# Second layer of a two-layer mixer on one core: both halves of a split operand as one moving operand of 512 columns, and the bank evacuated by a ScalarE copy

## The chip, the cores and the metric

The kernel runs on one core of a Trainium2 chip. The metric is the time of one execution in microseconds on the device; the kernel before has a median of 1196.91 us over three runs (1196.71 to 1197.09). Beside these runs one execution was profiled, and every row below is from that execution. Its granted TensorE clock is 1.0 in every slice, the 2.4 GHz level.

## The reference

Two layers of a diffusion backbone run over 256 latent and 256 context tokens of width 2048. In each layer the modulated RMS norm of the tokens goes through one input projection, whose columns are split among two branches and their gates; the gated branches are joined and go through one output projection. Only the latent stream leaves, so the context stream of the second layer is used for keys and values alone. Cut to what matters here, for the latent tokens of one layer:

```
h = rms_norm(x) * (1 + scale) + shift
u, v, za, q, k, vv, zb = split(h @ w_in)
a = gelu(u) * (w_sgu @ rms_norm(gelu(v)) + b_sgu) * silu(za)      # position mixing in chunks of 128
b = softmax(rope(norm(q)) @ rope(norm(k)).T / sqrt(128)) @ vv * silu(zb)   # 8 query heads, 2 key heads
x = x + gate * (concat(a, b) @ w_out)
```

## The kernel before

All large products are float32 products made of float32r passes: each operand is split into `hi` (its value rounded to float32r) and `lo` (what remains), and a product is three passes, hi by hi, hi by lo and lo by hi, that add up in one PSUM bank (`three`, lines 339 to 341).

A *job* is 512 output columns of a projection. Its weights come in 8 pieces of 256 rows by DMA; ScalarE makes a piece's `hi` (L202), VectorE its `lo` (L205), three pieces ahead of their use. In a job of kind "tok" tokens are the output's partitions; in a job of kind "feat", feature-major, 128 features are the partitions, the weights are the stationary operand and the tokens the moving one. The second layer's last part works on the 256 latent tokens alone, so its "feat" jobs move 256 columns per pass. There are ten such jobs: six of the input projection, with which the gates are made (U0, U1 with gelu, ZA0, ZA1, ZB0, ZB1 with silu, in the order U0, ZA0, U1, ZA1, ZB0, ZB1, other jobs between), and four of the output projection. In each, every piece gives four feature blocks (fb 0 to 3) of two contraction steps. The moving operand is the modulated input `h1` in the gate jobs and the gated product `mx` in the output jobs.

The four feature blocks of a job have one PSUM bank each, from a pool of four, so that the next job's block takes the bank of the same number when that has been read. When a gate job's block is complete, `gate_evac` has ScalarE read the bank with the activation (L637) into a tile `act`, and a tick later VectorE multiplies the branch's buffer by it (L642). When an output job's block is complete, VectorE adds it, times the gate, to the residual `x1` from the bank (L975), and a tick later the result leaves by DMA.

Side work runs between the units of the jobs: `tick()` is called after two feature blocks (or one tile of tokens) and moves each task one step on; `later(k, f)` puts f's instructions k + 1 ticks further on. The tasks are the attention of the second layer, the modulation vectors on VectorE (L284), and the position mixing. Attention turns the queries (`qT`, split at L475 and L476), makes scores `s` (TensorE), their negative maximum `nmx` (VectorE, L534), the exponentials `p` (ScalarE, L537, with the sum `sm`), scales p by the reciprocal of the sum (ScalarE, L630), turns it (`tp`, TensorE L544), splits it into `pt` (L475, L476), and multiplies it with the values (`o`, TensorE).

The order of instructions on each engine is that in which this program writes them, and every engine works through its own in order. Tiles of [128, 512] that live shortly (`act`, the split queries qT, p, squares, modulated rows) are taken in turn from one pool, tag "t2", of five buffers: a tile that takes a buffer waits until all readers of its previous tile are done.

Of the kernel before, what the change touches and what calls it, by code (L numbers as in the profile page):

```python
# [63 lines left out]
def mixer_kernel(ctx: ExitStack, tc: tile.TileContext, a, out):  # L64
    """Tokens are ordered latent (tiles 0, 1), context (tiles 2, 3).

    Every large product runs as three float32r passes over exact splits of both
    operands: v = hi + lo with hi = float32r(v), and a*b = hi*hi + hi*lo + lo*hi.
    """
# [67 lines left out]
    # the conditioning vectors behind their SiLU, in rows: (quarter, stream, element)  # L137
# [23 lines left out]
    def consts_task(l, L):  # L161
        """What the mixer needs beside the modulation: norm weights, and those of queries and keys with the rotation."""
# [34 lines left out]
    def split_piece(rs, at_once, mem=None):  # L197
        """float32r parts of two contraction blocks; the second part follows a tick later unless at once."""
        n = rs.shape[1]
        hi = hlp.tile([P, 2, 512], F32R, tag="hi", name=nm("hi"))[:, :n] if mem is None else mem[:, 0]  # L200
        lo = hlp.tile([P, 2, 512], F32R, tag="lo", name=nm("lo"))[:, :n] if mem is None else mem[:, 1]
        S.copy(hi, rs)  # L202

        def rest():
            V.tensor_tensor(out=lo, in0=rs, in1=hi.bitcast(F32), op=ALU.subtract)  # L205
        if at_once:
            rest()
        else:
            later(0, rest)
        return hi, lo  # L210

    class ModItems:
        """Shift and scale of n blocks of features from block kt0, for both streams, on the tensor engine: four
        steps over the contraction, then a finish."""
# [41 lines left out]
    def mod_task(row0, ng, ns, pace, finish):  # L256
        """ng groups of 256 columns of the modulation product on the vector engine, columns on the partitions.
        finish gets the sums [P, 2 * ng, ns] of the first ns streams."""
# [42 lines left out]
    def mod_rest():  # L301
        """The gates of the first layer, then the second layer's modulation."""
        yield from mod_task(0, 8, 2, MOD_PACE[0], mod_gate(L0, 2))
        yield from mod_task(D, 16, 2, MOD_PACE[1], lambda tot: mod_ab(L1, tot[:, :KT], tot[:, KT:], 0, KT))
        yield from mod_task(3 * D, 8, 1, MOD_PACE[2], mod_gate(L1, 1))

# [1 line left out]
    # A task is a generator; it yields how many units of the main stream pass before it goes on.  # L308
# [5 lines left out]
    def later(k, f):  # L314
        """Emit f's instructions k + 1 ticks from now."""
        def once():
            f()
            return
            yield
        spawn(once(), k)  # L320
# [21 lines left out]

    class Job:
        """512 output columns: units of main-stream work for each piece of two contraction blocks."""

        def __init__(self, W, col0, kind, n, operand, evac, order=(0, 1, 2, 3), pre=None, post=None, heavy=False):
            self.W, self.col0, self.kind, self.n = W, col0, kind, n
            self.operand, self.evac, self.order = operand, evac, order
            self.pre, self.post, self.heavy = pre, post, heavy
            self.ps = {}  # L350

        def units(self, i, pc):
# [13 lines left out]
            for fb in range(4):  # L366
                if first:
                    self.ps[fb] = accp.tile([P, 512], F32, tag="acc", name=nm("acc"))
                ps = self.ps[fb][:, :self.n]
                fs = slice(fb * P, (fb + 1) * P)  # L370
                for k in range(2):
                    three(ps, (pc[0][:, k, fs], pc[1][:, k, fs]), self.operand(kt0 + k),
                          first and k == 0, last and k == 1)
# [9 lines left out]
    class Stream:  # L383
        """The pieces of a list of jobs in order, loaded and split ahead of their use."""
# [50 lines left out]
    def head_norm(q, n, kind):  # L435
        """q [P, n, 128] in place: divide by the root mean square of each head."""
# [41 lines left out]
    def attention_task(L, kv, qa, units, done):  # L478
        """kv [P, 4, 512]: k heads in columns 0..255, v heads in 256..511. qa[hf] [P, nt, 4, 128]: queries in,
        transposed attention output in the same place."""  # L480
# [152 lines left out]
    def gate_evac(func, buf, ntok, mix=None):  # L633
        """buf [P, nt, 4, 128] *= func(product), block fb of 128 features; split if that was the last factor."""
        def f(fb, ps):
            t_ = t2([P, 512], "act")[:, :ntok]
            S.activation(t_, ps, func)  # L637
            b = buf[:, :, fb, :]


# [4 lines left out]
            later(0, mul)  # L645
        return f

    def to_mix(buf, mix, fb):
        """Split block fb of a finished [P, nt, 4, 128] buffer into float32r parts [P, 4, tokens]."""
# [6 lines left out]
    def sgu_v(L, buf, hf, nt):  # L656
        """buf [P, nt, 4, 128] gets the position-mixed value path, transposed."""
# [57 lines left out]
    def modulate(L, kt, stream, xs, rb, hi, lo):  # L715
        """hi + lo = xs * rb * A + B for one block of 128 features; returns what makes lo."""
# [7 lines left out]
    # column starts of the combined projection  # L724
    U0, VS0, ZA0, Q0, KV0, ZB0 = 0, 1024, 2048, 3072, 4096, 4608

    # ================= layer 0 =================
# [5 lines left out]
    def mod_load():  # L733
        """Loads modulation weights ahead, into at most MOD_AHEAD buffers."""
# [22 lines left out]
    def stats(s, g):  # L757
        """Mean squares of a stream's tokens; the tensor engine adds up over the features on the partitions."""
# [51 lines left out]
    def rows_h(gi):  # L810
        """Space for the modulated rows of a group, and the steps that make them."""
# [33 lines left out]
    def first_group():  # L845
        """The latent tokens' products run while the other stream arrives."""
# [114 lines left out]
    # the residual stream is read again for the output projection  # L961
# [42 lines left out]
    # layer 1 jobs  # L1004
# [4 lines left out]
    def rhs1(kt):  # L1009
        return h1[0][kt // 8][:, kt % 8, :], h1[0][2 + kt // 8][:, kt % 8, :]  # L1010

    def lhs1(kt, tt):
        hh = h1[tt // NLAT]
        ts = slice((tt % NLAT) * P, (tt % NLAT + 1) * P)
        return hh[kt // 8][:, kt % 8, ts], hh[2 + kt // 8][:, kt % 8, ts]
# [29 lines left out]
    def gate_job1(col0, func, buf, g=None):  # L1045
        def ev(fb, ps):
            assert ("sgu", 1, col0 // 512 % 2) in emitted or col0 >= ZB0
            if g is not None and fb == 0:
                assert g < 2 or g - 2 in done1
                t_ = big([P, 2, 4, SEQ], F32R, s="mx")  # L1050
                MX[g] = (t_[:, 0], t_[:, 1])
# [3 lines left out]
    def mix1(kt):  # L1055
        return MX[kt // 4][0][:, kt % 4, :], MX[kt // 4][1][:, kt % 4, :]

    def out_job1(cn):
        def ev(fb, ps):
            kt = 4 * cn + fb  # L1060
            xs = resid(L1, kt, 0, ps)
            later(0, lambda: nc.sync.dma_start(out=out[kt * P:(kt + 1) * P, :], in_=xs))
        return Job(a["w_out"][1], 512 * cn, "feat", SEQ, mix1, ev)
# [19 lines left out]
    # last columns of layer 0: the latent tokens end first, so that their next layer can begin  # L1083
# [18 lines left out]
    def next_task(s):  # L1102
        """The next layer's input of one stream, from the new residual stream."""
# [19 lines left out]
        for kt in range(KT):  # L1123
            if kt % 8 == 0:
                hs[kt // 8] = big([P, 8, SEQ], F32R, s="h1")
                hs[2 + kt // 8] = big([P, 8, SEQ], F32R, s="h1")
            assert ("mod", D) in emitted
            nxt = modulate(L1, kt, s, x1[s][kt // 8][:, kt % 8, :], rb, hs[kt // 8][:, kt % 8, :],
                           hs[2 + kt // 8][:, kt % 8, :])
# [37 lines left out]
    # ================= layer 1 =================  # L1167
# [6 lines left out]
def _layout(inputs):  # L1174
# [22 lines left out]
    # constants of the shapes alone  # L1197
# [33 lines left out]
```

## Time and profile before

| what | value |
|---|---|
| median of three runs | 1196.91 us |
| profiled execution, own time | about 1196.9 us: span and 2.3 us around it |
| span of the profile | 1194.6 us |
| TensorE busy | 1169.5 us, 98% of the span, 6656 matmuls and turns |
| VectorE busy | 908.9 us, 76% |
| ScalarE busy | 521.5 us, 44% |
| GpSimd busy | 47.0 us, 4% |

The span is the time from the first to the last instruction in the profile. Busy time of an engine says how much of the span its instructions cover; on TensorE consecutive matmuls overlap, so the distance of two starts, not one matmul's duration, is what a matmul costs in a stream. The second layer's "feat" jobs end at about 930 (U0), 961 (ZA0) and 1023 us (U1) while attention runs beside them, and follow each other without it from about 1045 us to the end.

### The profile page before, as it was taken

To read this page: it belongs to the slowest core of one execution; us is meant where nothing else is said; L and a number is where in the kernel's file an instruction comes from. 1 tells how busy PE (TensorE), PEld (TensorE's weight loads), DVE (VectorE), ACT (ScalarE), POOL (GpSimd) and SP (SyncE) were. 2 spreads that over 40 slices of the span, in tenths; PEclk is the share of its full clock that TensorE was granted. 3 is DMA by queue.
4 is the path that set the end of the run, shared out by engine and by line. 5 is a ranking of instruction groups with operands and counts; after the bars stand their busy time and mean duration, and the time that the engine had idled before them with its cause. 6 is when DMAs were issued, how large, how long until landed. Compare 5 with 4: busy or idle time off the path is not lost.

```text
span 1194.6 us, 18034 instructions
## 1 busy us (share of the span) xinstructions
PE 1169.5 (98%) x6656; PEld 991.5 (83%) x6656; DVE 908.9 (76%) x1930; ACT 521.5 (44%) x992; POOL 47.0 (4%) x48
## 2 busy tenths in 40 slices
PE   4999999999999999999999999999999999999998
PEld 2566667888888888888888888987888989999998
DVE  5767769878887777989988998778558687767544
ACT  4422225565555432242332232146366777645332
POOL 1000001011000000010100000000011000000000
PEclk9999999999999999999999999999999999999999
DMA  9986772446354657677786666646456666677752
GB/s 334 345 291 246 264 290 99 145 130 191 117 159 141 178 179 224 192 232 219 253 299 215 215 203 195 229 118 220 139 161 200 216 195 220 207 258 252 236 190 89
DMA packets 132184, 247.52 MB, mean 207 GB/s; under 512 B 8912, under 2 KB 19696, under 8 KB 132096
## 3 DMA queue, kind: packets, MB, share of 16 engines
q1 hardware_dynamic: 130880, 242.08, 62.3%
q0 software_dynamic: 1216, 4.29, 1.0%
q8 instruction: 52, 0.85, 0.3%
q14 instruction: 36, 0.29, 0.1%
HBM read 244.23 MB, written 2.11 MB: 206 GB/s over the span
## 4 chain that ended last, share of the span: by engine, by line
PE 89%; DVE 4%; ACT 3%; issue 1%; SPq 1%; POOL 1%; DMA 1%; POOLq 0%; ACTq 0%; DVEq 0%
PE acc L339 27%; PE acc L341 26%; PE acc L340 26%; PE mod L234 2%; PE tp L544 1%; DVE lo L205 1%; PE sg L686 1%; PE s L341 1%; ACT hi L202 1%; PE o L340 1%; PE o L341 1%; PE o L339 1%; POOL rs L429 1%; PE s L340 1%; PE s L339 1%
## 5 line engine op out<-in xcount | busy, mean ns | idle before, releaser
L202 ACT CAST hi<-raw 128x1024 fp32r<-128x1024 f32 (+1 forms) x242 | 250.7, 1036 | 395.6 <-PE acc L340 283.2
L205 DVE TENSOR_TENSOR lo<-raw,hi 128x1024 fp32r<-128x1024 f32 (+1 forms) x242 | 292.2, 1208 | 126.8 <-ACT hi L202 126.5
L284 DVE SCALAR_TENSOR_TENSOR junk<-raw,scb 128x512 f32<-128x512 f32 x448 | 308.1, 688 | 14.5 <-DMA raw<-in_w_modt 5.5
L339 PE MATMUL acc<-hh,hi 128*128 128x512 f32 x384 | 152.6, 397 | 0.0
L341 PE MATMUL acc<-hh,lo 128*128 128x512 f32 x384 | 149.8, 390 | 0.0
L340 PE MATMUL acc<-hl,hi 128*128 128x512 f32 x384 | 149.8, 390 | 0.0
L339 PE MATMUL acc<-hi,hh 128*128 128x512 f32 x320 | 131.0, 409 | 3.1 <-ACT hh L720 3.1
L341 PE MATMUL acc<-hi,hl 128*128 128x512 f32 x320 | 125.6, 393 | 0.0
L340 PE MATMUL acc<-lo,hh 128*128 128x512 f32 x320 | 125.3, 392 | 0.0
L339 PE MATMUL acc<-h,hi 128*128 128x256 f32 x384 | 110.3, 287 | 1.0 <-ACT s L660 1.0
L341 PE MATMUL acc<-h,lo 128*128 128x256 f32 x384 | 108.6, 283 | 0.0
L340 PE MATMUL acc<-h,hi 128*128 128x256 f32 x384 | 108.5, 283 | 0.0
L339 PE MATMUL acc<-mh,hi 128*128 128x512 f32 (+1 forms) x304 | 106.5, 350 | 0.0
L341 PE MATMUL acc<-mh,lo 128*128 128x512 f32 (+1 forms) x304 | 106.4, 350 | 0.0
L340 PE MATMUL acc<-ml,hi 128*128 128x512 f32 (+1 forms) x304 | 106.4, 350 | 0.0
L339 PEld LDWEIGHTS acc<-hi,hh 128*128 128x128 f32 x320 | 60.5, 189 | 38.8 <-issue 14.7
L341 PEld LDWEIGHTS acc<-hh,lo 128*128 128x128 f32 x384 | 72.1, 188 | 15.4
L340 PEld LDWEIGHTS acc<-hl,hi 128*128 128x128 f32 x384 | 72.3, 188 | 13.5
L339 PEld LDWEIGHTS acc<-hh,hi 128*128 128x128 f32 x384 | 72.2, 188 | 13.5
L429 POOL TENSOR_TENSOR rs<-rs,nhalf 128x4 f32<-128x4 f32 (+1 forms) x36 | 40.9, 1137 | 892.7 <-DVE rs L428 892.7
L340 PE MATMUL acc<-lo,h 128*128 128x512 f32 x192 | 75.3, 392 | 0.7 <-DVE lo L205 0.3
L339 PE MATMUL acc<-hi,h 128*128 128x512 f32 x192 | 75.7, 394 | 0.0
(163 smaller groups left out, 2166.6 us busy)
## 6 DMA issues: line engine op xcount, KB each, us to landing
raw<-in_w_in SPq DMA_DIRECT2D x173, 512.0 KB, 4.4
raw<-in_w_modt SPq DMA_DIRECT2D x128, 512.0 KB, 4.7
raw<-in_w_out SPq DMA_DIRECT2D x64, 512.0 KB, 5.0
raw<-in_w_mod SPq DMA_DIRECT2D x58, 512.0 KB, 6.2
scb<-crow SPq DMA_DIRECT2D x12, 512.0 KB, 6.0
xT<-in_xT SPq DMA_DIRECT2D x8, 512.0 KB, 7.8
x<-in_xT POOLq DMA_DIRECT2D x4, 1024.0 KB, 11.0
mod<-in_w_mod SPq DMA_DIRECT2D x6, 512.0 KB, 7.7
```

What stands on the lines that cost most here:

```text
L202: S.copy(hi, rs)
L205: V.tensor_tensor(out=lo, in0=rs, in1=hi.bitcast(F32), op=ALU.subtract)
L234: T.matmul(self.ps[32 * j:32 * j + 32, :wd], sc[:, 4 * g + j, :], self.raw[g][j], start=(g == 0), stop=(g == 3))
L284: V.scalar_tensor_tensor(out=junk, in0=rs[i][:, b_, :], scalar=1.0, in1=scbs[q][:, s_, :], op0=ALU.mult, op1=ALU.mult, accum_out=part[:, 2 ...
L339: T.matmul(ps, lhi, rhi, start=first, stop=False)
L340: T.matmul(ps, lhi, rlo, start=False, stop=False)
L341: T.matmul(ps, llo, rhi, start=False, stop=last)
L429: G.tensor_tensor(out=r, in0=r, in1=nhalf[:, :n], op=ALU.pow)
L544: T.transpose(out=tp[:, c * P:(c + 1) * P], in_=p_[:, c * P:(c + 1) * P], identity=ident)
L686: T.matmul(ps[:, tt * P:(tt + 1) * P], buf[:, tt, g, :], ws[:, g, :], start=True, stop=True)
```

## The change

The operands `h1` and `mx` are laid out so that the hi and lo halves of one contraction block lie beside each other, 512 columns in all. `paired` then makes a product of two matmuls: the weights' hi against the 512 columns [hi | lo] into a whole bank, and the weights' lo against the 256 columns of hi into the bank's first half. The sum of the bank's halves is the product.

So a gate job's block now leaves in four steps: ScalarE copies the 512 columns to a tile "both" of the pool t2; a tick later VectorE adds its halves into `act`; a tick later ScalarE applies the activation in place; a tick later VectorE multiplies. An output job's block is copied in the same way, and a tick later two residual adds read the two halves from SBUF. The last block of the last output job (`single=(3,)`) keeps the three passes and the add from PSUM. In the program TensorE has 624 matmuls fewer, ScalarE 39 copies and 5 table loads more, VectorE 24 tensor_tensor and 15 residual adds more.

```
+    def paired(ps, lh, rh, first, last):
+        (lhi, llo), n = lh, rh.shape[2]
+        T.matmul(view(ps, "p (o n) -> p o n", o=2), lhi, rh, start=first, stop=False)
+        T.matmul(ps[:, :n], llo, rh[:, 0], start=False, stop=last)
...
-                ps = self.ps[fb][:, :self.n]
+                pair = self.n < NTOK and fb not in self.single
+                ps = self.ps[fb][:, :2 * self.n if pair else self.n]
...
-                    three(ps, (pc[0][:, k, fs], pc[1][:, k, fs]), self.operand(kt0 + k),
-                          first and k == 0, last and k == 1)
+                    w, x = (pc[0][:, k, fs], pc[1][:, k, fs]), self.operand(kt0 + k)
+                    if pair:
+                        paired(ps, w, x, first and k == 0, last and k == 1)
+                    else:
+                        three(ps, w, x if self.n == NTOK else (x[:, 0], x[:, 1]), first and k == 0, last and k == 1)
...
     def gate_evac(func, buf, ntok, mix=None):
         def f(fb, ps):
             t_ = t2([P, 512], "act")[:, :ntok]
-            S.activation(t_, ps, func)
             b = buf[:, :, fb, :]
+            if ps.shape[-1] > ntok:
+                both = t2([P, 512], "both")
+                S.copy(both, ps)
+
+                def add():
+                    V.tensor_tensor(out=t_, in0=both[:, :ntok], in1=both[:, ntok:], op=ALU.add)
+                    later(0, act)
+                later(0, add)
+            else:
+                S.activation(t_, ps, func)
+                later(0, lambda: mul())
+
+            def act():
+                S.activation(t_, t_, func)
+                later(0, mul)
...
-            xs = resid(L1, kt, 0, ps)
-            later(0, lambda: nc.sync.dma_start(out=out[kt * P:(kt + 1) * P, :], in_=xs))
-        return Job(a["w_out"][1], 512 * cn, "feat", SEQ, mix1, ev)
+
+            def add(ps):
+                for h in range(0, ps.shape[-1], SEQ):
+                    xs = resid(L1, kt, 0, ps[:, h:h + SEQ])
+                later(0, lambda: nc.sync.dma_start(out=out[kt * P:(kt + 1) * P, :], in_=xs))
+            if ps.shape[-1] > SEQ:
+                both = t2([P, 512], "both")
+                S.copy(both, ps)
+                later(0, lambda: add(both))
+            else:
+                add(ps)
+        return Job(a["w_out"][1], 512 * cn, "feat", SEQ, mix1, ev, single=(3,) if cn == 3 else ())
```

What stands on the engines at the end of job U0 shows how the steps have moved. On ScalarE before, behind the last split of U0's stretch (acc_1401 to acc_1406 are U0's four banks; pt_1440 and p_1451 belong to one head, p_1469 and qT_1476 to the steps after it):

```order
L637 ACT_TABLE_LOAD
L637 ACTIVATE act_1458_8169<-acc_1401_7846 128x256
...
L637 ACTIVATE act_1461_8196<-acc_1406_7874 128x256
L475 CAST pt_1440_8063<-tp_1454_8153 128x4x128
L630 ACTIVATE p_1451_8134<-p_1451_8134,sm_1452_8135 128x512
L202 CAST hi_1462_8205<-raw_1445_8076 128x1024
L537 ACT_TABLE_LOAD
L537 ACTIVATE p_1469_8230,sm_1470_8231<-s_1467_8224,nmx_1468_8228 128x512
L202 CAST hi_1479_8274<-raw_1448_8114 128x1024
L558 COPY qa_1216_6875<-o_1474_8251 128x256
L475 CAST qT_1476_8267<-qt_1475_8264 128x256
```

And after, at the same place:

```order
L652 COPY both_1459_8112<-acc_1401_7846 128x512
...
L652 COPY both_1465_8136<-acc_1406_7868 128x512
L487 CAST pt_1440_8023<-tp_1454_8097 128x4x128
L642 ACTIVATE p_1451_8082<-p_1451_8082,sm_1452_8083 128x512
L663 ACT_TABLE_LOAD
L663 ACTIVATE act_1458_8111<-act_1458_8111 128x256
...
L549 ACT_TABLE_LOAD
L549 ACTIVATE p_1473_8168,sm_1474_8169<-s_1471_8162,nmx_1472_8166 128x512
L663 ACT_TABLE_LOAD
L663 ACTIVATE act_1462_8128<-act_1462_8128 128x256
L663 ACTIVATE act_1464_8135<-act_1464_8135 128x256
L202 CAST hi_1483_8214<-raw_1448_8066 128x1024
L570 COPY qa_1216_6875<-o_1478_8189 128x256
```

Four copies take the activations' place, and the activations stand in two pairs, one ahead of the exponentials and one behind them, so that three table loads stand where there were two, and a fourth follows for the next exponentials. As the buffers of the pool t2 come round, both_1463 takes that of a tile which the first adds read, and both_1465 that of qT_1439, whose last reader is TensorE's s_1471.

On VectorE before, at the same place, the products follow the activations:

```order
L205 TENSOR_TENSOR lo_1456_8159<-raw_1430_8014,hi_1455_8158 128x1024
L642 TENSOR_TENSOR s2_1344_7586<-s2_1344_7586,act_1458_8169 128x2x128
L642 TENSOR_TENSOR s2_1344_7586<-s2_1344_7586,act_1459_8177 128x2x128
L284 SCALAR_TENSOR_TENSOR junk_1177_6547,mpart_1176_6546<-raw_1340_7578,scb_1182_6556 128x512
L476 TENSOR_TENSOR pt_1440_8063<-tp_1454_8153,pt_1440_8063 128x4x128
L629 RECIPROCAL sm_1452_8135<-sm_1452_8135 128x1
```

And after:

```order
L205 TENSOR_TENSOR lo_1456_8103<-raw_1430_7982,hi_1455_8102 128x1024
L655 TENSOR_TENSOR act_1458_8111<-both_1459_8112 128x256
L655 TENSOR_TENSOR act_1460_8118<-both_1461_8119 128x256
L284 SCALAR_TENSOR_TENSOR junk_1177_6547,mpart_1176_6546<-raw_1340_7578,scb_1182_6556 128x512
L488 TENSOR_TENSOR pt_1440_8023<-tp_1454_8097,pt_1440_8023 128x4x128
L641 RECIPROCAL sm_1452_8083<-sm_1452_8083 128x1
L655 TENSOR_TENSOR act_1462_8128<-both_1463_8129 128x256
L655 TENSOR_TENSOR act_1464_8135<-both_1465_8136 128x256
L546 TENSOR_REDUCE nmx_1472_8166<-s_1471_8162 128x1
L667 TENSOR_TENSOR s2_1344_7586<-s2_1344_7586,act_1458_8111 128x2x128
L667 TENSOR_TENSOR s2_1344_7586<-s2_1344_7586,act_1460_8118 128x2x128
L205 TENSOR_TENSOR lo_1467_8148<-raw_1445_8036,hi_1466_8147 128x1024
```

The adds stand where the products stood, and the products two ticks further on, between nmx and the next lo.

At the end of the program the residual adds of the last output job stand on VectorE like this after the change (both_1926 to both_1928 are the copies of feature blocks 0 to 2, acc_1913 is the bank of block 3):

```order
L205 TENSOR_TENSOR lo_1925_10633<-raw_1919_10567,hi_1924_10632 128x1024
L999 SCALAR_TENSOR_TENSOR x1_1016_5324<-both_1926_10676,modG1_309_1392,x1_1016_5324 128x256 x2
L999 SCALAR_TENSOR_TENSOR x1_1016_5324<-both_1927_10682,modG1_309_1392,x1_1016_5324 128x256 x2
L999 SCALAR_TENSOR_TENSOR x1_1016_5324<-acc_1913_10533,modG1_309_1392,x1_1016_5324 128x256
L999 SCALAR_TENSOR_TENSOR x1_1016_5324<-both_1928_10692,modG1_309_1392,x1_1016_5324 128x256 x2
```

Before, four adds stood there, one for each bank in the order of the blocks; now block 2 comes last, with two.

## Rows read from the trace of the kernel before

**Rows 1.** Page, part 1: busy time, share of the span, count.

```profile
PE 1169.5 (98%) x6656; PEld 991.5 (83%) x6656; DVE 908.9 (76%) x1930; ACT 521.5 (44%) x992; POOL 47.0 (4%) x48
```

**Rows 2.** TensorE's groups by line and shape: count | busy us, mean ns.

```profile
L340 PE MATMUL acc<-h,hi 128*128 128x256 f32 x384 | 108.5, 283 | 0.0
...
L340 PE MATMUL acc<-mx,hi 128*128 128x256 f32 x256 | 72.5, 283 | 0.0
```

**Rows 3.** Timeline of TensorE, 512 columns: start, duration; first and last of 20.

```profile
869.67 0.39 PE L339 MATMUL acc<-hi,h 128*128 128x512 f32 x1
...
873.98 0.39 PE L340 MATMUL acc<-lo,h 128*128 128x512 f32 x1
```

**Rows 4.** Timeline of TensorE, 256 columns, a gate job; first and last of 28.

```profile
1069.75 0.28 PE L339 MATMUL acc<-h,hi 128*128 128x256 f32 x1
...
1072.99 0.28 PE L339 MATMUL acc<-h,hi 128*128 128x256 f32 x1
```

**Rows 5.** Windows: length, busy PE, PEld, DVE, ACT, POOL, clock, DMA share, GB/s.

```profile
980.00:1000.00 20.00, 20.00 (x127) 17.98 (x126) 15.51 (x29) 17.14 (x39) 2.01 (x2) 1.00 0.67 213
...
1045.00:1190.00 145.00, 145.00 (x1210) 144.96 (x1210) 84.93 (x129) 58.98 (x73) 0.00 (x0) 1.00 0.63 208
```

**Rows 6.** Line 1023: ScalarE's copies of a whole bank, min/median/max ns.

```profile
L1023 ACT COPY qa<-acc x4: 573/578/587, 832.0 to 835.9; 128x512 f32<-128x512 f32 x4
```

**Rows 7.** Timeline of ScalarE at U0's end: start, us, instruction [idle before <-releaser].

```profile
928.99 1.04 ACT L202 CAST hi<-raw 128x1024 fp32r<-128x1024 f32 x1
930.05 1.28 ACT L637 ACT_TABLE_LOAD   x1
931.34 1.37 ACT L637 ACTIVATE act<-acc 128x256 f32<-128x256 f32 x4
932.61 0.58 ACT L475 CAST pt<-tp 128x512 fp32r<-128x512 f32 x1
934.02 0.73 ACT L630 ACTIVATE p<-p,sm 128x512 f32<-128x512 f32 x1 [0.83 <-DVE sm L629]
...
936.99 0.69 ACT L537 ACTIVATE p<-s,nmx 128x512 f32<-128x512 f32 x1
...
938.87 0.38 ACT L475 CAST qT<-qt 128x256 fp32r<-128x256 f32 x1
```

**Rows 8.** Timeline of VectorE at U0's end.

```profile
936.85 0.68 DVE L284 SCALAR_TENSOR_TENSOR junk<-raw,scb 128x512 f32<-128x512 f32 x1
...
938.74 1.23 DVE L205 TENSOR_TENSOR lo<-raw,hi 128x1024 fp32r<-128x1024 f32 x1 [1.20 <-ACT hi L202]
939.88 0.42 DVE L476 TENSOR_TENSOR qT<-qt,qT 128x256 fp32r<-128x256 f32 x1
```

**Rows 9.** Timeline of TensorE behind U0's end: passes of two heads' scores.

```profile
934.04 0.39 PE L341 MATMUL s<-kT,qT 128*128 128x512 f32 x1
...
942.09 0.40 PE L339 MATMUL s<-kT,qT 128*128 128x512 f32 x1
...
942.56 0.39 PE L341 MATMUL s<-kT,qT 128*128 128x512 f32 x1
```

**Rows 10.** Timeline of VectorE and TensorE behind ZA0's end.

```profile
964.77 0.39 PE L341 MATMUL s<-kT,qT 128*128 128x512 f32 x1
...
971.96 0.42 DVE L476 TENSOR_TENSOR qT<-qt,qT 128x256 fp32r<-128x256 f32 x1
...
973.03 0.39 PE L341 MATMUL s<-kT,qT 128*128 128x512 f32 x1
```

**Rows 11.** Timeline of ScalarE and TensorE behind U1's end.

```profile
1027.18 0.39 PE L341 MATMUL s<-kT,qT 128*128 128x512 f32 x1
...
1033.86 0.72 ACT L630 ACTIVATE p<-p,sm 128x512 f32<-128x512 f32 x1 [1.26 <-DVE sm L629]
...
1036.46 0.60 PE L544 MATMUL tp<-ident,p 128*128 128x128 f32 x4
```

**Rows 12.** Timeline of VectorE at the end: the last residual add.

```profile
1191.26 0.48 DVE L975 SCALAR_TENSOR_TENSOR x<-acc,modG,x 128x256 f32<-128x256 f32 x1 [0.23 <-PE acc L341]
```

More of the change, by code (lines that the diff above doesn't have):

```diff
@@ L341, in three, with __init__ @@
         T.matmul(ps, llo, rhi, start=False, stop=last)
+    def paired(ps, lh, rh, first, last):
+        (lhi, llo), n = lh, rh.shape[2]
+        T.matmul(view(ps, "p (o n) -> p o n", o=2), lhi, rh, start=first, stop=False)
+        T.matmul(ps[:, :n], llo, rh[:, 0], start=False, stop=last)
     class Job:
-        def __init__(self, W, col0, kind, n, operand, evac, order=(0, 1, 2, 3), pre=None, post=None, heavy=False):
+        def __init__(self, W, col0, kind, n, operand, evac, order=(0, 1, 2, 3), pre=None, post=None, heavy=False, single=()):
+            self.single = single
             self.W, self.col0, self.kind, self.n = W, col0, kind, n
@@ L644, in mul @@
                     later(MIX_LAG, lambda: to_mix(buf, mix, fb))
-            later(0, mul)
         return f
@@ L1009, in rhs1 @@
     def rhs1(kt):
-        return h1[0][kt // 8][:, kt % 8, :], h1[0][2 + kt // 8][:, kt % 8, :]
+        return h1[0][kt // 4][:, kt % 4]
     def lhs1(kt, tt):
@@ L1014, in lhs1 @@
         ts = slice((tt % NLAT) * P, (tt % NLAT + 1) * P)
-        return hh[kt // 8][:, kt % 8, ts], hh[2 + kt // 8][:, kt % 8, ts]
+        return hh[kt // 4][:, kt % 4, 0, ts], hh[kt // 4][:, kt % 4, 1, ts]
     def q_job1(hf):
@@ L1049, in ev @@
                 assert g < 2 or g - 2 in done1
-                t_ = big([P, 2, 4, SEQ], F32R, s="mx")
-                MX[g] = (t_[:, 0], t_[:, 1])
+                t_ = big([P, 4, 2, SEQ], F32R, s="mx")
+                MX[g] = (t_[:, :, 0], t_[:, :, 1], t_)
             gate_evac(func, buf(), SEQ, None if g is None else MX[g])(fb, ps)
@@ L1055, in mix1 @@
     def mix1(kt):
-        return MX[kt // 4][0][:, kt % 4, :], MX[kt // 4][1][:, kt % 4, :]
+        return MX[kt // 4][2][:, kt % 4]
     def out_job1(cn):
@@ L1123, in next_task @@
         for kt in range(KT):
-            if kt % 8 == 0:
-                hs[kt // 8] = big([P, 8, SEQ], F32R, s="h1")
-                hs[2 + kt // 8] = big([P, 8, SEQ], F32R, s="h1")
+            if kt % 4 == 0:
+                hs[kt // 4] = big([P, 4, 2, SEQ], F32R, s="h1")
             assert ("mod", D) in emitted
-            nxt = modulate(L1, kt, s, x1[s][kt // 8][:, kt % 8, :], rb, hs[kt // 8][:, kt % 8, :],
-                           hs[2 + kt // 8][:, kt % 8, :])
+            nxt = modulate(L1, kt, s, x1[s][kt // 8][:, kt % 8, :], rb, hs[kt // 4][:, kt % 4, 0],
+                           hs[kt // 4][:, kt % 4, 1])
             rest()
```

## Prediction

> **What bounds the kernel now.** The page's first part comes first: TensorE is busy 98% of the span [rows 1], and the span (1194.6 us of the execution's 1196.9) is about what its matmuls take, one behind another. A matmul fewer, or a shorter one, is worth its full time, unless TensorE must then wait. The groups by line and shape say how many are touched [rows 2]: in the ten jobs of the change, each of the three passes of `three` runs 384 times against the modulated input and 256 times against the gated product, so there are 640 triples of 128x256. Their busy time (283 ns each) is no price, since matmuls overlap; the timeline gives the distance of their starts. 19 steps between matmuls of 512 columns take 4.31 us, 226.8 ns each [rows 3]; 27 steps at 256 columns take 3.24 us, 120.0 ns each [rows 4]. Twice 120.0 is 13.2 ns more than 226.8: what a matmul costs beside its columns.
>
> Then the windows: which other engine is near its limit, and where [rows 5]? From 1045 us (ZA1 to the end) ScalarE works 59 and VectorE 85 of 145 us. Between 980 and 1000 us, where attention runs beside the jobs, ScalarE works 17.1 and VectorE 15.5 of 20. So work added to these two is hidden at the end and questionable in the attention stretch, which holds the ends of three changed jobs: U0 (930 us), ZA0 (961 us), U1 (1023 us).
>
> **What TensorE saves.** A triple takes 3 x 120.0 = 360.0 ns; a pair takes 226.8 + 120.0 = 346.8 ns. All 640 but the 16 of the last feature block are paired: 624 x 13.2 ns = 8.2 us. The attention's own 512-column passes stand 235 ns apart (0.47 us for two steps, [rows 9]); at that pace a pair takes 355 ns, and the saving is 624 x 5 = 3.1 us. I take 8.2, since rows 3 are matmuls of a large product, as these are, and keep 3.1 as the bound.
>
> One rule speaks against it: the Trainium skill, "TensorE: Matmul & The Clock Gate", section "Back-to-back issue gap", puts an isolated warm matmul at N/2.4 + 2.5 ns, so that dropping one returns only 2.5 ns. By it the saving would be 624 x 2.5 ns = 1.6 us. Rows 3 and 4 disagree: 13.2 ns beside the columns.
>
> **What is added, and where it is hidden.** Each of the 39 paired feature blocks leaves by a ScalarE copy of the whole bank (0.58 us, [rows 6]) instead of an activation (1.37/4 = 0.34 us, [rows 7]); the 24 of the gate jobs then cost a VectorE add (0.42 us for a 256-column tensor_tensor, [rows 8]) and the activation again from SBUF; the 15 of the output jobs a second residual add (0.48 us, [rows 12]). In ZA1, ZB0, ZB1 and the output jobs both engines idle about half the time [rows 5], banks are free as early as before (0.58 after each 0.69 of TensorE), and I cost this at nothing. If that cover were gone it would be at most 4 x 0.58 us at each of seven job ends.
>
> **Where it isn't hidden.** Each "both" tile takes a buffer of the pool of five that the attention steps use as well; and as the activations come later than the next exp, ScalarE loads its tables alternately: five loads more in all (two at U0, two at ZA0, one about U1), 1.28 us each, the next activation starting 0.01 us behind [rows 7].
>
> A second rule would make that worse: the Trainium skill, "ScalarE: Activation LUTs", section "What ACT_TABLE_LOAD costs", adds 1.38 us of drain to a load of 1.28. The trace shows the 1.28 and no drain [rows 7]; with it, five loads would cost ScalarE 6.9 us more.
>
> *End of U0.* Before, the four activations follow hi at once and end at 932.7 [rows 7]. Now ScalarE copies both_0 at 930.05, both_1 at 930.75, and both_2 by 932.0 once the first two adds returned a buffer. both_3 takes the buffer of qT, which TensorE still reads for the second head's scores; those stand behind two feature blocks of the next job, so the copy waits until the scores end. Before that was 934.04 + 0.39 = 934.43 [rows 9]; with some fifteen pairs of 13 ns saved since the evacuation began, 934.2. Everything behind it on ScalarE, which works in order, starts from there: both_3 to 934.8; pt cast 0.58 to 935.35 (before 932.61); then pt's low half and the reciprocal on VectorE, 0.83 as before, and p's scaling 0.73 to 936.85; table load to 938.1; two activations to 938.75; hi 1.04 to 939.75; table load to 941.05; exp 0.69 to 941.85; table load to 943.1; the other two activations to 943.75; hi to 944.75; a short copy; and qT's cast at 944.9 where it was 938.87. On VectorE lo (1.23) ends at 946.0 and qT's low half (0.42) at 946.4; before, 939.88 + 0.42 = 940.30 [rows 8]. The third pass of the next scores needs that half. It started at 942.56 [rows 9], so the slack was 2.26 us; with the savings it would start at about 942.05. TensorE waits **4.35 us**. Two smaller stops in front of it (the value product for pt, some 0.4; the lo of a piece, some 0.5) lie inside, since the same wait follows.
>
> *End of ZA0.* Here both_2 already waits for the scores, so two copies follow them instead of one, and VectorE has a step of the modulation (0.68 us, [rows 8]) between the last gate product and lo. From the scores' end, 964.77 + 0.39 [rows 10] less 0.25 saved, the chain of U0 (946.4 - 934.2 = 12.2 us) plus 0.5 plus 0.6 (neighbours on an engine overlap by 0.1) gives 978.2 for qT's low half. It was done at 972.38 and needed at 973.03: only 0.65 us of slack [rows 10]. Nominally needed now at 972.8: a wait of 5.4. One head later the value product needs a pt that now stands behind one more table load and four casts to mx in one block where two and two were; read the same way, about 1.0 more (an estimate; bounds 0 and the 1.28 of that load). **6.4 us**.
>
> *End of U1.* both_3 again waits for the scores, 1027.18 + 0.39 [rows 11], now about 1027.35. To the second hi the chain is U0's (944.75 - 934.2 = 10.55), so 1037.9; then the short copy (0.3, a little under an activation of its size), pt's cast 0.58, VectorE's part 0.83 and p's scaling 0.72: it ends at 1040.35, where it ended at 1034.58. The turning of p on TensorE was at 1036.46 [rows 11], a slack of 1.9; it would now be at 1035.95. **4.4 us**.
>
> *Tail.* Before, the last residual add starts at 1191.26 [rows 12]. Now fb 3's single add precedes fb 2's two in VectorE's order, so the last transfer starts two overlapped adds later: **0.9 us**.
>
> **Sum.** -8.2 + 4.35 + 6.4 + 4.4 + 0.9 = +7.85 us on this execution's 1196.9, which is also the median of the runs: **1204.8 us**. The three waits are bounded below by zero (if ScalarE and VectorE use their idle time, as the 0.83 us before p's scaling in rows 7, to catch up) and above by the chains read with another 1.28 us each.
>
> **Rivals.** *A, the waits are half as long.* If the buffers' waits free sooner, or lo and qT change places with idle time, each chain shortens by 2 to 3 us. Stalls of 6 to 11 us pay off the saving: 1195 to 1200, say 1197.5. For: VectorE is idle 4.5 of 20 us there. Against: the chain runs mostly through ScalarE, in order.
>
> *B, the other side: faster.* ScalarE's lateness at the three places stays within the slack (2.26, 0.65, 1.9 us). Then only saving and tail count: 1196.9 - 8.2 + 0.9 = 1189.6. It decides at the fourth copy: if the buffer taken there is free before the scores, copies cost 4 x (0.58 - 0.34) = 1 us and U0 and U1 stay covered. Against: the order names the buffer's reader, and two table loads alone are 2.56 us.
>
> *C, worse.* After a stop, the following heads' steps come late too (splits of weights have a few us of lead, but one engine makes all of them), so that each place costs 2 us more: 1209 to 1213. A rule of a dearer table load would end here too: 2 x 1.38 us further at each chain of two loads, 1204.8 + 3 x 2.76 = 1213; as rows 7 show no such drain, I give it 0.02.
>
> *D, pairing saves nothing like 8 us.* If a 512-column step took as long as two of 256 less 2.5 ns, the sum would be 1204.8 + 6.6 = 1211.4. Rows 3 and 4 leave it 0.02.
>
> **Chances.** Forecast 0.60 (its own range 1200 to 1208), A 0.17, B 0.11, C and D 0.12. The range of 8 in 10 reaches to A's low end and into C: 1195.5 to 1209.5. A measurement tells 0.2%, 2.4 us, from no change. Faster: B and a little of A, 0.14. Same: most of A, 0.14. Slower: 0.72.
>
> **What would show it.** In the profile after, starts of pairs 227 and 120 ns apart, and TensorE's matmul count down by 624. On ScalarE the fourth copy at the ends of U0 and U1, the third at ZA0, with an idle time released by TensorE's s; on TensorE waits of 4 to 6 us for qT's low half (twice) and for p (once). The last 145 us without waits, 6 us shorter. I would be wrong if those copies do not wait, if ScalarE's table loads number fewer than five more, or if TensorE's waits stay under 2 us each.

## The result and the profile after

The changed kernel takes 1212.9 us (median of four runs, 1211.03 to 1215.22) where the kernel before takes 1196.9 beside it: a ratio of 1.0133, 95% interval 1.0121 to 1.0144. It is slower, as forecast, but by twice the 7.85 us of the forecast, and outside its range. The profiled execution is the slowest of the four, 1215.22 us. The page's first part, which answers to [rows 1], and its line of granted clocks:

```profile
span 1213.3 us, 16867 instructions
PE 1176.2 (97%) x6032; PEld 963.4 (79%) x6032; DVE 923.6 (76%) x1969; ACT 549.9 (45%) x1036; POOL 47.0 (4%) x48
PEclk9999999999999999999999999999999889999999
```

TensorE has 624 matmuls fewer and is yet busy 6.7 us longer. Two slices have a granted clock under 0.9, which no slice of the kernel before has. The largest waits of TensorE from 700 us on (what waits <- for what: us, times, longest; the others are 1.0 us or less in all):

```profile
PE s L339 <- ACT qT L487: 4.8, 2, 2.4
PE tp L556 <- ACT p L642: 3.3, 1, 3.3
PE acc L340 <- DVE lo L205: 1.4, 2, 1.1
```

The wait for qT twice and the one for p once stand at the three places that were forecast. ScalarE's timeline behind U0, which answers to [rows 7], tells how they come about; the last two lines are the copies that wait for the scores behind ZA0 and U1:

```profile
930.72 1.30 ACT L652 COPY both<-acc 128x512 f32<-128x512 f32 x2
932.82 0.59 ACT L652 COPY both<-acc 128x512 f32<-128x512 f32 x1 [0.81 <-DVE act L655]
934.96 0.59 ACT L652 COPY both<-acc 128x512 f32<-128x512 f32 x1 [1.55 <-PE s L341]
935.44 0.59 ACT L487 CAST pt<-tp 128x512 fp32r<-128x512 f32 x1
936.86 0.72 ACT L642 ACTIVATE p<-p,sm 128x512 f32<-128x512 f32 x1 [0.83 <-DVE sm L641]
937.60 1.28 ACT L663 ACT_TABLE_LOAD   x1
938.89 0.73 ACT L663 ACTIVATE act<-act 128x256 f32<-128x256 f32 x2
...
940.71 1.28 ACT L549 ACT_TABLE_LOAD   x1
...
942.80 1.28 ACT L663 ACT_TABLE_LOAD   x1
...
945.92 0.37 ACT L487 CAST qT<-qt 128x256 fp32r<-128x256 f32 x1
...
972.20 1.07 ACT L652 COPY both<-acc 128x512 f32<-128x512 f32 x2 [2.87 <-PE s L341]
...
1041.83 0.58 ACT L652 COPY both<-acc 128x512 f32<-128x512 f32 x1 [1.53 <-PE s L341]
```

Behind U0 the third copy waits for VectorE's adds, the fourth for the scores; three table loads follow, and qT's cast starts 7.05 us later than in [rows 7]. What follows on TensorE was not foreseen. The windows (columns as in [rows 5]):

```profile
944.00:946.00 2.00, 0.00 (x0) 0.00 (x0) 0.98 (x3) 1.99 (x6) 0.00 (x0) 0.97 0.64 230
946.00:950.00 4.00, 3.66 (x10) 2.72 (x11) 3.42 (x8) 2.66 (x6) 0.00 (x0) 0.50 0.45 125
...
984.00:990.00 6.00, 5.30 (x14) 3.93 (x15) 4.91 (x10) 4.60 (x8) 0.00 (x0) 0.50 0.55 173
1055.00:1058.00 3.00, 2.70 (x10) 2.42 (x11) 1.81 (x6) 2.60 (x4) 0.00 (x0) 0.52 0.86 257
```

Behind each of the three waits the granted clock is 0.50 for some microseconds, the level of 1.2 GHz, and the starts stand further apart: a pair behind U0 takes 640 ns (512-column starts at 948.63, 949.27 and 949.91), where one at full clock takes 353 (below). The mean clock of the four runs goes with their times: 1215.22 us at 0.992, 1214.30 at 0.994, 1211.51 and 1211.03 at 0.997. So the profiled execution is the one with the most time at half clock.

The pace of the pairs, in the late part where nothing waits (a gate job; first and last of 13 matmuls):

```profile
1109.84 0.40 PE L347 MATMUL acc<-h,hi 128*128 128x512 f32 x1
...
1111.96 0.40 PE L347 MATMUL acc<-h,hi 128*128 128x512 f32 x1
```

Six pairs take 2.12 us, 353.3 ns each. That is 6.6 ns less than three passes at 120.0, half of the 13.2 that were forecast.

A ledger of the difference comes from the start of the same TensorE step in both profiles. The *lag* is how much later that step starts after the change (for instance the scores at 933.57 before and 934.05 after, a lag of 0.48). How the lag changes, in us:

| stretch, by the time of the kernel before | change of the lag |
|---|---|
| start to 891.4 (nothing in it is changed) | +0.92 |
| 891.4 to 933.6: U0's pairs | -0.44 |
| 933.6 to 949.0: behind U0 | +6.74 |
| 949.0 to 964.3 | -0.23 |
| 964.3 to 979.2: behind ZA0 | +7.95 |
| 979.2 to 1026.7 | -0.71 |
| 1026.7 to 1042.7: behind U1 | +5.94 |
| 1042.7 to the last matmul | -2.72 |
| last matmul to the end | +1.24 |
| sum, 1213.3 - 1194.6 | +18.7 |

### The profile page after: what moved, and what is told of

Read it like the earlier page. It is cut to its first block, busy times and chain, and to the rows that moved or that the text cites. A ratio compares the mean times of both kernels' runs of the same rounds, so it can differ in the third digit from the quotient of the medians.

```text
span 1213.3 us, 16867 instructions
## 1 busy us (share of the span) xinstructions
PE 1176.2 (97%) x6032; PEld 963.4 (79%) x6032; DVE 923.6 (76%) x1969; ACT 549.9 (45%) x1036; POOL 47.0 (4%) x48
## 4 chain that ended last, share of the span: by engine, by line
PE 86%; DVE 5%; ACT 5%; issue 2%; DMA 1%; POOL 1%; SPq 0%; ACTq 0%; DVEq 0%; POOLq 0%
PE acc L339 20%; PE acc L341 19%; PE acc L340 19%; PE acc L347 11%; PE acc L348 6%; PE mod L234 3%; PE tp L556 1%; DVE lo L205 1%; ACT hi L202 1%; PE sg L710 1%; PE s L341 1%; POOL rs L441 1%; PE o L340 1%; PE s L339 1%; PE o L341 1%
## 5 line engine op out<-in xcount | busy, mean ns | idle before, releaser
L339 PE MATMUL acc<-hh,hi 128*128 128x512 f32 x384 | 152.7, 398 | 0.0
L347 PE MATMUL acc<-h,hi 128*128 128x512 f32 x384 | 141.2, 408 | 1.0 <-ACT s L684 1.0
L339 PE MATMUL acc<-hi,hh 128*128 128x512 f32 x320 | 131.5, 411 | 3.1 <-ACT hh L744 3.1
L339 PE MATMUL acc<-mh,hi 128*128 128x512 f32 (+1 forms) x304 | 106.5, 350 | 0.0
L339 PEld LDWEIGHTS acc<-hi,hh 128*128 128x128 f32 x320 | 60.5, 189 | 39.2 <-issue 15.5
L347 PEld LDWEIGHTS acc<-h,hi 128*128 128x128 f32 x384 | 73.7, 192 | 18.6 <-ACT s L684 1.3
L347 PE MATMUL acc<-mx,hi 128*128 128x512 f32 x240 | 85.2, 399 | 0.0
L339 PEld LDWEIGHTS acc<-hh,hi 128*128 128x128 f32 x384 | 72.2, 188 | 13.5
L339 PE MATMUL acc<-hi,h 128*128 128x512 f32 x192 | 76.4, 398 | 0.0
```

The costliest lines, as they stand in the source:

```text
L339: T.matmul(ps, lhi, rhi, start=first, stop=False)
L347: T.matmul(view(ps, "p (o n) -> p o n", o=2), lhi, rh, start=first, stop=False)
```

## Experiments

The ratios below are to the kernel before, with 95% intervals in brackets. The reasons to be told apart: **places** (the loss is made where the evacuation meets the attention, by buffers, by table loads, or by the work itself), **clock** (the half clock behind the waits is a loss of its own), **pace** (why a pair takes 353 ns), and their rival, that the pairs or the copies cost time wherever they stand. The kernel before ran beside all of them, at medians from 1196.8 to 1197.3 us.

**Late jobs alone (pair_late_jobs).**

```
-    rest += [..., gate_job1(U0 + 512 * hf, GELU, ...), gate_job1(ZA0 + 512 * hf, SILU, ..., hf)]
+    rest += [..., gate_job1(U0 + 512 * hf, GELU, ..., single=(0, 1, 2, 3)),
+             gate_job1(ZA0 + 512 * hf, SILU, ..., hf, single=() if hf else (0, 1, 2, 3))]
```

> Only ZA1, ZB0, ZB1 and the output jobs are paired; U0, ZA0 and U1 keep three passes and the old evacuation. Theory (the loss is made where the evacuation meets the attention): no wait of TensorE for qT or p, granted clock 1.0, and 432 pairs that save 6.6 ns each (353.4 ns as the changed kernel's profile shows them, not 346.8): 2.9 us less, 1.2 us more at the tail, 1195.2 us. Rival (the pairs themselves or the copies cost the time wherever they stand): seven tenths of the loss stay, about 1208 us.

Measured: 1195.32 us, ratio 0.9984 (0.9975 to 0.9993). The lag does not change at any of the three places (0.00, 0.00, -0.23), the late part gains 2.71 and the tail loses 1.24, as in the changed kernel; that is the time of the theory. So the pairs do no harm by themselves, and the whole loss comes from pairing U0, ZA0 and U1.

**TensorE kept busy in the waits (busy_in_waits).**

```
+        def keep_busy(t_, n_):
+            for _ in range(n_):
+                T.matmul(t_[:, :256], kT[:, 0, 0, :P], kT[:, 0, 0, :256], start=True, stop=True)
```

called on the bank of the scores (20 times, two heads) and of the turned p (28 times, once).

> The changed kernel with matmuls without use (128 by 256 into the bank that the scores or the turned p overwrite afterwards) where TensorE waits: 20 ahead of the scores behind U0 and behind ZA0, 28 ahead of the turning behind U1, 2.4, 2.4 and 3.4 us of the waits seen. The result is unchanged. Theory (each long wait is followed by some us at half the clock, which costs 3.3, 3.4 and 1.8 us): the operands come as late as before, but the granted clock stays at 1.0 and the time falls by about 8 from the profiled 1215.2, to about 1206.7 us. Rival (the clock falls for another reason, or the slow matmuls hide behind late operands anyway): clock 0.992 to 0.997 again and 1211 to 1215 us.

Measured: 1211.14 us, ratio 1.0116 (1.0099 to 1.0132), clock 0.999 to 1.0 in all four runs. The stretches behind the three waits, where the clock was 0.50, are at full clock:

```profile
946.00:952.00 6.00, 5.66 (x36) 4.70 (x35) 4.85 (x10) 4.65 (x9) 0.00 (x0) 1.00 0.44 136
982.00:988.00 6.00, 5.59 (x33) 4.46 (x32) 4.78 (x10) 4.62 (x9) 0.00 (x0) 1.00 0.68 225
1049.00:1056.00 7.00, 7.00 (x51) 6.43 (x51) 4.30 (x8) 5.72 (x10) 0.00 (x0) 1.00 0.54 159
```

The three places now cost 4.36, 5.92 and 4.55 us instead of 6.74, 7.95 and 5.94: the half clock cost 5.8 us there. That the time falls by less has two reasons. Between ZA0 and U1 the lag grows by 0.90 where it shrank by 0.71, since TensorE, not slowed, now waits for pt. And this profile is 2.42 us late before any changed instruction (see the last experiment). By the profiles' spans (1213.3 and 1210.6), less the lags at 891 us, the half clock is worth 4.1 us in the profiled execution. By the medians (1212.9 and 1211.14) it is 1.8 us, and the two intervals overlap: the profiled execution of the changed kernel has more time at half clock than the other three. So the theory holds for the clock and not for the 8 us. The time is in the rival's range, and a part of its reason holds: some of the slow time would have been waited for anyway.

**Own buffers, and one table turn.** Two edits apart and then together. own_buffers:

```
-                both = t2([P, 512], "both")
+                if fb == 0:
+                    BOTH[:] = [big([P, 4, 512], s="both")]
+                both = BOTH[0][:, fb]
```

> The changed kernel, but the copies of a gate job go to a tile of their own (four tiles in one large buffer) and not to the pool that attention uses. Theory A (buffers and table loads each make about half of ScalarE's lateness): no copy waits for the scores, qT's cast behind U0 comes about 3 us earlier, TensorE's waits fall to 1 to 1.5 us at U0 and U1 and about 3 at ZA0, fewer falls of the clock: about 1202 us. Rival B (the waits of the copies are all): no waits of TensorE, about 1195 us. Rival C (table loads and the work itself are all): 1209 us or more.

one_table_turn:

```
-                    later(0, act)
+                    later(0 if fb > 1 else 1, act)
```

> The changed kernel, but the activations of the first two feature blocks come a tick later, with those of the last two, so that the tables are loaded 21 times in the program instead of 27; the copies still take buffers of the attention's pool. Theory A (buffers and loads each about half): qT's cast behind U0 about 3 us earlier than 945.9, waits of TensorE of 1 to 2 us, fewer falls of the clock: about 1202 us. Rival B (buffers are all): 1209 us or more. Rival C (loads are all): about 1195 us.

own_and_one_turn, both edits:

> Both edits at once: the gate jobs' copies in a tile of their own, and the four activations together a tick later. Theory A (buffers first, table loads second, nothing else): qT's cast behind U0 at about 941, qT's low half before TensorE needs it, no wait at U0 and U1, 0 to 1.5 us at ZA0, clock 1.0; 4.1 us of saving less 1.2 of tail and what is left at ZA0: 1194.5 to 1196.5 us beside 1197.3 before. Rival (the extra work of ScalarE and VectorE, 0.24 us a copy and 0.4 an add, makes the lateness too): waits of 2 us and more stay and the time is 1200 us or more.

Measured, with the change of the lag at the three places:

| kernel | median us | ratio to before | behind U0 | ZA0 | U1 |
|---|---|---|---|---|---|
| changed | 1212.9 | 1.0133 (1.0121 to 1.0144) | 6.74 | 7.95 | 5.94 |
| one_table_turn | 1211.84 | 1.0125 (1.0109 to 1.0140) | 6.12 | 7.63 | 5.26 |
| own_buffers | 1205.13 | 1.0066 (1.0051 to 1.0081) | 2.18 | 4.68 | 2.44 |
| own_and_one_turn | 1200.50 | 1.0031 (1.0019 to 1.0043) | 1.39 | 1.92 | 1.48 |

Buffers and loads are not halves: theory A's 1202 us came in neither kernel. With the buffers kept, six loads fewer gain next to nothing, and the waits of that kernel say why (925 to 1062 us, VectorE's and then ScalarE's):

```profile
DVE act L655 <- PE tp L556: 6.8, 3, 2.3
```

```profile
ACT p L549 <- DVE nmx L546: 13.5, 9, 2.8
ACT both L652 <- PE s L341: 5.8, 3, 2.9
```

The second adds write to a buffer whose p TensorE has yet to turn; nmx stands behind them on VectorE, and ScalarE's exp behind nmx. In the changed kernel the add waits as long (6.8), but exp and the load ahead of it only 6.6 us. So 6.9 us more are waited for now, and six loads of 1.28 us are 7.7: most of what the loads gave back went into this wait. Only with the copies out of the pool do the loads count: 4.6 us between own_buffers and own_and_one_turn (4.2 by the ratios). The clock has a part in these, since own_buffers still has a fall of it behind ZA0 and the other none. The third forecast, no wait at U0 and U1, missed by 4 us, and the time is in its rival's range. What is left there is not the extra work of that rival, as the next experiment shows, but a buffer again (ScalarE, 925 to 1045 us):

```profile
ACT p L549 <- PE tp L556: 5.3, 3, 2.0
```

The activations come a tick later, their tiles hold buffers of the pool longer, and p takes one that TensorE still reads.

**No buffer of the pool at all (all_own_one_turn).** The add and the activation work in the copy's own tile:

```
-            t_ = t2([P, 512], "act")[:, :ntok]
+                t_ = both[:, :ntok]
```

> As the kernel with own buffers and one table turn, but the halves are added in place and the activation works there too, so that a gate job takes no buffer of the attention's pool at all. In that kernel's profile ScalarE's exp still waits 1.8 us at each of the three places until TensorE has turned a p whose buffer it takes. Theory (what was left is this third wait for a buffer): TensorE's waits for qT and p vanish or stay under 0.5 us, 4.5 to 5 us less than its 1200.5: about 1195.5 us. Rival (ScalarE's and VectorE's extra work is too much for the places even so): waits of 1 us each stay, 1199 us or more.

Measured: 1196.01 us, ratio 0.9988 (0.9979 to 0.9997); the three places change the lag by -0.29, +0.48 and -0.24. TensorE's waits from 860 us on, beside one of 1.0 us that the kernel before has as well:

```profile
PE s L341 <- DVE qT L488: 0.8, 2, 0.7
PE o L340 <- DVE pt L488: 0.6, 1, 0.6
```

One of 0.5 us for qT, ahead of U0's end, is in the kernel before as well. The 0.6 for pt, behind ZA0, is new, and between ZA0 and U1 the lag grows by 0.93 where the pairs should make it shrink. So the 24 copies and 24 adds fit beside the attention but for some 1.8 us of lag behind ZA0 (from 964 to 1005 us). It was the buffers, and with the copies out of the pool the loads, that did not. Whether the loads cost anything once no tile is in the pool was not tried.

**A copy of half a bank (half_copy).**

```
-                both = t2([P, 512], "both")
-                S.copy(both, ps)
...
+                S.copy(t_, ps[:, ntok:])
+                V.tensor_tensor(out=t_, in0=ps[:, :ntok], in1=t_, op=ALU.add)
+                later(0 if fb > 1 else 1, lambda: act())
```

with t_ in a tile of its own.

> All ten jobs paired; a gate job's block leaves by a ScalarE copy of the bank's second half alone (256 columns, 0.34 us) into a tile of its own, VectorE adds the first half from PSUM at once, and the four activations come together a tick later. Theory A: ScalarE's work at a job's end is 1 us less than with whole copies, no wait for qT or p; 1194 to 1196 us. Rival (the banks are now freed by VectorE, behind a lo of 1.2 us): TensorE waits 0.3 to 1 us for a bank at each of the six gate jobs, 1197 to 1200 us.

Measured: 1199.75 us, ratio 1.0026 (1.0015 to 1.0037). The time is in the rival's range, but neither theory's reason holds: TensorE waits for a bank twice, 0.2 us each, and yet loses 1.37, 1.76 and 1.61 us at the three places. In ScalarE's timeline the activations stand ahead of the exp again, with a table load on either side of them; p's scaling waits 1.73 us for VectorE, whose adds stand ahead of pt:

```profile
935.68 0.72 ACT L642 ACTIVATE p<-p,sm 128x512 f32<-128x512 f32 x1 [1.73 <-DVE sm L641]
936.42 1.28 ACT L664 ACT_TABLE_LOAD   x1
937.72 1.34 ACT L664 ACTIVATE own<-own 128x256 f32<-128x256 f32 x4
...
940.01 1.28 ACT L549 ACT_TABLE_LOAD   x1
```

How much each has of it was not tried apart.

**The order of the passes (late_jobs_hi_hi_lo_lo).** Late jobs alone, and in a unit of two contraction blocks:

```
+                    for k in range(2):
+                        T.matmul(view(ps, "p (o n) -> p o n", o=2), pc[0][:, k, fs], xs[k], start=first and k == 0, stop=False)
+                    for k in range(2):
+                        T.matmul(ps[:, :self.n], pc[1][:, k, fs], xs[k][:, 0], start=False, stop=last and k == 1)
```

> Late jobs alone paired, as in the first experiment, with the passes of a unit's two contraction blocks in another order: both 512-column matmuls, then both of 256. Theory P (the 6.6 ns that a pair takes above 226.8 + 120.0 belong to the change of shape at every matmul): a unit of two pairs takes about 700 instead of 707 ns, and 216 such units save 1.5 us more, about 1193.8 us. Rival (the extra belongs to the 512-column matmul with its two halves, or to the bank): 707 ns again and 1195.3 us.

Measured: 1193.48 us, ratio 0.9969 (0.9958 to 0.9981). Two units, by the starts of their 512-column matmuls:

```profile
1110.07 0.63 PE L383 MATMUL acc<-mx,hi 128*128 128x512 f32 x2
...
1111.46 0.63 PE L383 MATMUL acc<-mx,hi 128*128 128x512 f32 x2
```

1.39 us for two, 695 ns a unit instead of 707; the late part gains 4.75 us where it gained 2.71, 9 ns a unit on the mean. So the order costs something: this one is faster than shapes in turn. 695 is about the 693.6 of the forecast's steps, but not by its parts: a 512-column step takes about 233 ns, whether one of 512 or one of 256 follows, and one of 256 about 115, against 226.8 and 120.0. So theory P has the time, but the 512-column step stays longer without a change of shape, as its rival has it. Why is open.

**The tail (late_jobs_best), and all jobs in the same order (all_jobs_best, all_own_best).** The last output job keeps three passes:

```
-        return Job(..., single=(3,) if cn == 3 else ())
+        return Job(..., single=(0, 1, 2, 3) if cn == 3 else ())
```

> ZA1, ZB0, ZB1 and the first three output jobs paired with the order hi, hi, lo, lo; the last output job entirely in three passes, with its adds from PSUM. Theory: the tail returns to that of the kernel before (1.2 us less than now), and the 48 feature-block steps that are no longer paired in the last job give back 48 x 11 ns = 0.5 us; beside the 1193.5 of the same order without this: 1192.5 to 1193.0 us. Rival (the last copies were hidden and the tail belongs to the transfer): no gain from the tail, 1194 us.

Measured: 1192.43 us, ratio 0.9962 (0.9948 to 0.9975), the lowest median of all. The tail is that of the kernel before, 3.65 us from the last matmul's start. In the changed kernel VectorE is still at the adds of blocks 0 and 1 when block 3 is done, and ends with two more adds, which start 0.40 us behind block 3's:

```profile
1207.21 1.92 DVE L999 SCALAR_TENSOR_TENSOR x<-both,modG,x 128x256 f32<-128x256 f32 x4 [4.82 <-ACT both L1092]
1209.05 0.48 DVE L999 SCALAR_TENSOR_TENSOR x<-acc,modG,x 128x256 f32<-128x256 f32 x1
1209.45 1.00 DVE L999 SCALAR_TENSOR_TENSOR x<-both,modG,x 128x256 f32<-128x256 f32 x2
```

> As the kernel with own buffers and one table turn, with the order hi, hi, lo, lo and the last output job in three passes. Theory: the waits behind U0, ZA0 and U1 stay at 1 to 2 us each, the order saves 3 us and the tail 0.7 beside its 1200.5: 1196.5 to 1197.5 us, no better than the kernel before and 4 us behind the kernel that pairs late jobs alone. Rival (the waits shift away with the faster units): below 1194 us.

Measured (own buffers for the copies, one turn): 1197.59 us, ratio 1.0005 (0.9996 to 1.0014); places 1.37, 1.92, 1.47, as expected.

> The same with the order hi, hi, lo, lo and the last output job in three passes. Theory: 3 us less than without, 1192 to 1193 us, about the same as pairing the late jobs alone in that order (1192.4), since the early jobs' 192 pairs give 2.1 us less what small waits take. Rival (waits stay): 1196 us or more.

Measured: 1193.04 us, ratio 0.9966 (0.9954 to 0.9979). The intervals of this and of the late jobs alone cover each other: pairing the early jobs is worth nothing that could be measured, even with no tile in the pool. Not every wait is gone: from 891 to 964 us the lag falls by 1.15 us, as the pairs should make it, and from there to 1005 us it grows by 1.9, behind waits for qT (0.24) and pt (0.57) behind ZA0.

**The kernel before, profiled again (before_again).**

> The kernel before once more, for a second profile of it. Theory: the 0.5 to 1.5 us by which all profiles with the change run late at 826 us, ahead of every changed instruction, come from a piece of weights that arrives late by chance; a second profile of the kernel before then shows a distance of 3.4 to 4.7 us between rs and rsb at 822 us instead of 3.23. Rival (the new layout of h1 makes it): 3.2 us again.

Measured: 1197.73 us. Its rs and rsb, on TensorE:

```profile
822.95 0.50 PE L1113 MATMUL rs<-ones,sums 128*128 128x1 f32 x4
826.93 0.68 PE L704 MATMUL rsb<-dg,ones 128*128 128x128 f32 x4 [0.60 <-DVE dg L696]
```

3.98 us apart where the first profile has 3.23, and the changed kernel's 3.73. A lag at 826 us comes in the kernel before too; the +0.92 of the ledger needs no change to explain it.

## Why the prediction was wrong

*The waits.* Right in place and number, and near in size. The fourth copy waited for the scores at U0 and U1 and the third at ZA0; qT's cast came 7.05 us late where the walk had 6.0, and 0.5 of the 7.05 is the lag that the execution brought along. The walk had TensorE wait at the scores' third pass, for qT's low half; the wait is at the first pass (L339), for the cast itself, and with the clock kept at 1.0 only 0.32 us (U0) are waited for the low half. Without the fall of the clock the three places cost 4.4, 5.9 and 4.6 us; forecast were 4.35, 6.4 and 4.4, of which the 1.0 for pt came later, as 0.8 us of lag between ZA0 and U1.

*The clock: a step that was missing.* The sum let TensorE go on at its pace behind each wait. It went on at half the granted clock: 5.8 us at the three places, 4.1 net in the profiled execution, 1.8 by the medians.

*The saving: the term that was mis-sized.* "A triple takes 3 x 120.0 = 360.0 ns; a pair takes 226.8 + 120.0 = 346.8 ns" took each shape's pace from a stream of that shape alone. In turn they take 353.3, and 624 x 6.6 ns = 4.1 us of saving where 8.2 were forecast: the other 4.1 us are the largest miss in the median. The last 145 us were to be 6 us shorter; from 1042.7 us to the last matmul it is 2.72, for 392 pairs. The bound of 3.1, from the 235 ns of [rows 9], was nearer than the value taken. The Trainium skill's 2.5 ns ("TensorE: Matmul & The Clock Gate", section "Back-to-back issue gap", for an isolated matmul) is not what the trace shows either: 6.6 ns come back per matmul dropped, and 12.5 in the better order (two triples are 720 ns, the unit of two pairs 695).

*The tail.* 0.9 forecast, 1.24 measured. The two added adds behind block 3's are the 0.9; the rest is that block 3's own add starts 0.65 us behind the last matmul's start where it was 0.31, as VectorE is still at blocks 0 and 1.

*The rest.* The profiled execution is 17.8 us longer than the kernel before from 891 us on. With pace, clock and tail put right the sum is 7.85 + 4.1 + 4.1 + 0.3 = 16.4 us. What is left, 1.4 us, is about what busy_in_waits also has beyond 7.85 + 4.1 + 0.3 (13.6 us from 891 us on), so the waits were somewhat longer than forecast, chiefly behind ZA0. The median is 16.0, as the clock fell for less time in the other executions. The two main faults, pace and clock, lie on the same side, so a range wide enough for the waits was too narrow.

Of the rivals, C names a time (1209 to 1213) that holds the measured one, but by luck: its reason, that the following heads come late too, shows at full clock only behind ZA0; what was lost beyond the forecast's waits, 5.5 us at the three places of the profiled execution, is the half clock. B saw only half of its point of decision: own_buffers frees the buffer at the fourth copy, and U0 and U1 still cost 2.2 and 2.4 us; they are covered when the loads and the other buffers are out of the way as well, as all_own_one_turn shows. C's dearer table load was rightly given little: in the timeline behind U0 the activations start at 938.89, 0.01 us behind the load's end.

## What to carry to other kernels

A tile that a change adds to a shared pool is a wait in the making: follow for each of its buffers who reads it last, and what stands behind the instruction that waits. Price a wait of a busy TensorE with what the clock does after it, and price a mixed stream of matmuls from a mixed stream. An evacuation that costs nothing where the engines idle can cost more than the whole gain in the few microseconds where they do not; pair, or convert, only the jobs that have room.

## What the runs showed of the hardware

The fall of the granted clock was the surprise. Idle stretches of TensorE of 2.7 us (U0), 2.8 us (ZA0) and 3.6 us (U1), counted from start to start, were each followed by 0.50 in the windows above. In own_and_one_turn none was longer than 1.9 us, and the clock stayed (0.999). It is no matter of the wait's length alone: in own_buffers the stretch of 2.5 us behind ZA0, counted in the same way, was followed by a fall, the longer one of 2.9 us behind U1 by none:

```profile
976.00:984.00 8.00, 6.72 (x23) 5.17 (x24) 6.28 (x14) 6.61 (x14) 0.00 (x0) 0.79 0.55 170
1042.00:1050.00 8.00, 5.43 (x33) 4.59 (x32) 6.42 (x11) 5.25 (x8) 0.00 (x0) 1.00 0.59 160
```

Matmuls without use in the waits kept it at 1.0. The other surprise is that a stream of two shapes in turn is slower than the sum of its parts (353.3 ns a pair beside 346.8), and that the order within a unit of two pairs gives 9 to 12 of its 707 ns back.
